# Gate and up projections of three FFNs as seven block products instead of eight

## The chip, the cores and the metric

The kernel runs on one core of one Trainium2 chip. The metric is the time on the device, in microseconds, from the start to the end of one execution. The core has a matrix engine (TensorE; PE in the views, with its weight loads as PEld) and three engines for everything else: VectorE (DVE), ScalarE (ACT) and GpSimd (POOL). SyncE (SP) issues most DMAs, GpSimd issues the rest. The engines run side by side, each one its own queue of instructions in order, and wait for one another by semaphores.

## The reference

Two layers of a transformer block over 512 image tokens (A) and 256 context tokens (C), width 1024, all in float32. Each layer has two FFNs of inner width 2816 around a stage of four mixers:

```python
def swiglu(h, wg, wu, wd):
    return (jax.nn.silu(h @ wg) * (h @ wu)) @ wd
...
    for i in range(DEPTH):
        need_ctx = i < DEPTH - 1
        mx = modulation(c, ada_w[i], ada_b[i])
        mc = modulation(c_ctx[None, :], ada_w[i], ada_b[i])
        x = x + 0.5 * mx[2] * swiglu(pre_norm(x, norm1_g[i], mx[0], mx[1]), ffn1_wg[i], ffn1_wu[i], ffn1_wd[i])
        xc = xc + 0.5 * mc[2] * swiglu(pre_norm(xc, norm1_g[i], mc[0], mc[1]), ffn1_wg[i], ffn1_wu[i], ffn1_wd[i])
        ...
        x = x + mx[5] * (jnp.concatenate([ya, yd, ym, yn], axis=-1) @ w_out[i])
        x = x + 0.5 * mx[8] * swiglu(pre_norm(x, norm3_g[i], mx[6], mx[7]), ffn2_wg[i], ffn2_wu[i], ffn2_wd[i])
        if need_ctx:
            ...
```

So four FFNs run one behind the other. Three of them are on image and context together: both of layer 0 and the first of layer 1. The last one is on the image alone. `modulation` is a product of a vector with a 1024 x 9216 matrix; its nine slices (j = 0 to 8) scale, shift and gate the norms and FFNs.

## The kernel before

Activations lie transposed, with the 1024 features as KD = 8 chunks of 128 partitions and the tokens along the free dimension. Every large product is done as three float32r matmuls (`mm3`, lines 290 to 292): each operand is split into a rounded high part and the rest (hi by ScalarE at L269, lo = src - hi by VectorE at L274), and high x high, high x low and low x high are added in PSUM.

`ffn` loops over 22 blocks f of 128 hidden features. For a block it loads the gate and the up weights (two tiles `wr` of 128 x 1024, by SyncE), splits them, and runs 8 chunks x 3 matmuls x 2 (gate and up) on the context (256 columns, bank `guC`) and on the image (512 columns, banks `gA`, `uA`). ScalarE makes silu of the gate (L326), VectorE multiplies (L327) and both split the result into `hh` and `hl`. After every group of 5 or 6 blocks (`GROUPS`) the down projection runs: for each of 8 chunks m of output features a weight tile is loaded and split, the matmuls of the group go to `dacc`, and VectorE adds the result, scaled by the gate column, into the residual X (L348). In the last group this is done token part by token part (`PASSES`), so that the norm of a part (`norm`, L260, L263, L264: `nt`, then `xnh` and `xnl`) can run while the next part is multiplied.

The modulation runs beside the FFNs as a generator (`ada`) of which `fill` takes a few steps per block: GpSimd's queue loads weight tiles `adaw` (L133), and VectorE multiplies each by two columns and accumulates into four tiles `adaacc` (L159, L161). `adasum` adds them over the partitions on TensorE.

The program is written in this order, and a scheduler of the framework places the instructions of each engine by a timeline of its own; the order on the chip is fixed when the program is built.

## Time and profile before

| what | value |
|---|---|
| time, median of 3 runs | 3256.35 us (3253.59 to 3258.81) |
| the profiled execution: its time | 3254.35 us |
| its span, first to last instruction | 3252.6 us |
| mean granted TensorE clock | 0.977 of full speed |
| PE, DVE, ACT, POOL busy | 96%, 53%, 33%, 14% of the span |

Times of a timeline are counted from the start of the span. A matmul's duration runs into that of the next (they are pipelined), so the price of a matmul in a stream is the distance between two starts. In the same way two VectorE instructions overlap by some hundredths of a microsecond where neither waits.

### The profile page before, as it was taken

How to read it: one execution, taken by the hardware profiler on the slowest of the kernel's cores; microseconds unless marked ns; L12 is line 12 of the kernel's file. 1: busy time of each engine (PE TensorE's matmuls, PEld its weight loads, DVE VectorE, ACT ScalarE, POOL GpSimd, SP SyncE). 2: the span in 40 equal slices, each digit the busy share in tenths (PEclk: the TensorE clock that was granted, in tenths of full speed). 3: DMA queues.
4: the chain of work that ended last, by engine and by line, in shares of the span. 5: the costliest groups of instructions: out<-in, count | busy, mean ns of one | idle time of the engine just before them, and what ended most of it. 6: DMA issues, size and time to landing. Idle time of an engine off the chain costs nothing.

```text
span 3252.6 us, 48912 instructions
## 1 busy us (share of the span) xinstructions
PE 3129.6 (96%) x19586; PEld 2713.3 (83%) x19586; DVE 1715.9 (53%) x3044; ACT 1069.6 (33%) x1927; POOL 463.6 (14%) x772
## 2 busy tenths in 40 slices
PE   7999999998999999999999999999997899999998
PEld 4888888886788889888889988888886688788887
DVE  5746354836855477675736332322746744353334
ACT  3212112555444433121224212122455353342223
POOL 2201010411232021121102000000311322000001
PEclk9999999999999999999999999999998999899999
DMA  6534242514533354454424221212523623323333
GB/s 244 153 104 138 87 117 81 168 62 124 159 91 87 89 191 131 142 153 126 128 77 123 63 64 59 72 53 67 148 78 114 162 57 81 121 86 96 97 97 104
DMA packets 135396, 357.45 MB, mean 110 GB/s; under 512 B 20000, under 2 KB 33824, under 8 KB 134912
## 3 DMA queue, kind: packets, MB, share of 16 engines
q1 hardware_dynamic: 101056, 255.47, 25.9%
q0 software_dynamic: 34112, 98.85, 11.0%
q8 instruction: 154, 2.52, 0.3%
q14 instruction: 74, 0.61, 0.1%
HBM read 316.89 MB, written 39.65 MB: 110 GB/s over the span
## 4 chain that ended last, share of the span: by engine, by line
PE 57%; DVE 4%; issue 3%; DMA 2%; ACT 1%; POOL 0%; POOLq 0%; DVEq 0%; SPq 0%; ACTq 0%
PE dacc L290 4%; PE dacc L292 4%; PE dacc L291 4%; PE gA L290 4%; PE gA L291 4%; PE uA L290 4%; PE uA L292 4%; PE uA L291 4%; PE gA L292 4%; PE guC L292 3%; PE guC L290 3%; PE guC L291 3%; PE o L740 2%; PE pj L290 1%; PE pj L292 1%
## 5 line engine op out<-in xcount | busy, mean ns | idle before, releaser
L269 ACT CAST wh<-wr 128x1024 fp32r<-128x1024 f32 (+5 forms) x443 | 394.7, 893 | 1239.4 <-PE dacc L291 453.3
L274 DVE TENSOR_TENSOR wl<-wr,wh 128x1024 fp32r<-128x1024 f32 (+5 forms) x443 | 461.2, 1043 | 422.6 <-ACT wh L269 391.6
L290 PE MATMUL dacc<-hh,wh 128*128 128x256 f32 (+1 forms) x1392 | 452.5, 326 | 2.2 <-ACT wh L269 1.9
L292 PE MATMUL dacc<-hh,wl 128*128 128x256 f32 (+1 forms) x1392 | 450.4, 326 | 3.6 <-DVE wl L274 3.5
L291 PE MATMUL dacc<-hl,wh 128*128 128x256 f32 (+1 forms) x1392 | 452.2, 326 | 0.0
L161 DVE SCALAR_TENSOR_TENSOR adaacc<-adaw,silc,adaacc 128x512 f32<-128x512 f32 x448 | 315.4, 748 | 12.2 <-DMA adaw<-ada_w 11.8
L290 PE MATMUL guC<-xnhC,wh 128*128 128x256 f32 x1056 | 300.2, 285 | 1.6 <-ACT xnhC L263 1.5
L291 PE MATMUL guC<-xnlC,wh 128*128 128x256 f32 x1056 | 299.5, 284 | 1.5 <-DVE xnlC L264 1.5
L292 PE MATMUL guC<-xnhC,wl 128*128 128x256 f32 x1056 | 299.0, 283 | 0.5 <-DVE wl L274 0.5
L290 PEld LDWEIGHTS dacc<-hh,wh 128*128 128x128 f32 x1392 | 261.4, 188 | 32.0 <-ACT wh L269 6.1
L290 PE MATMUL gA<-xnhA,wh 128*128 128x512 f32 (+1 forms) x752 | 284.8, 379 | 1.7 <-ACT xnhA L263 1.7
L292 PEld LDWEIGHTS dacc<-hh,wl 128*128 128x128 f32 x1392 | 261.0, 188 | 29.6 <-DVE wl L274 5.0
L290 PE MATMUL uA<-xnhA,wh 128*128 128x512 f32 (+1 forms) x752 | 283.0, 376 | 0.6 <-ACT wh L269 0.6
L292 PE MATMUL uA<-xnhA,wl 128*128 128x512 f32 (+1 forms) x752 | 282.8, 376 | 0.7 <-DVE wl L274 0.7
L291 PE MATMUL uA<-xnlA,wh 128*128 128x512 f32 (+1 forms) x752 | 282.9, 376 | 0.0
L292 PE MATMUL gA<-xnhA,wl 128*128 128x512 f32 (+1 forms) x752 | 282.8, 376 | 0.0
L291 PE MATMUL gA<-xnlA,wh 128*128 128x512 f32 (+1 forms) x752 | 282.2, 377 | 0.0
L291 PEld LDWEIGHTS dacc<-hl,wh 128*128 128x128 f32 x1392 | 261.4, 188 | 24.6
L133 POOL DMA_DIRECT2D adaw<-ada_w x256 | 140.6, 550 | 799.2 <-DVE adaacc L159 483.3
L348 DVE SCALAR_TENSOR_TENSOR xA<-dacc,modG,xA 128x512 f32<-128x512 f32 (+1 forms) x160 | 101.9, 640 | 239.3 <-PE dacc L292 239.2
L290 PEld LDWEIGHTS guC<-xnhC,wh 128*128 128x128 f32 x1056 | 202.7, 192 | 9.5 <-ACT wh L269 5.2
L291 PEld LDWEIGHTS guC<-xnlC,wh 128*128 128x128 f32 x1056 | 202.6, 192 | 4.4 <-DVE xnlC L264 2.0
(354 smaller groups left out, 5944.9 us busy)
## 6 DMA issues: line engine op xcount, KB each, us to landing
wr<-wgu SPq DMA_DIRECT2D x176, 512.0 KB, 3.6
adaw<-ada_w POOLq DMA_DIRECT2D x256, 256.0 KB, 3.3
wr<-wd SPq DMA_DIRECT2D x120, 320.0 KB, 3.0
wr<-wd SPq DMA_DIRECT2D x64, 384.0 KB, 3.2
wr<-win SPq DMA_DIRECT2D x44, 512.0 KB, 3.9
...
```

The costliest lines, as they stand in the source:

```text
L133: load = lambda q, t, k, c: q.dma_start(out=t, in_=self.I["ada_w"][l, k * 128:(k + 1) * 128, c:c + 512])
L161: nc.vector.scalar_tensor_tensor(out=t, in0=w, scalar=c, in1=t, op0=ALU.mult, op1=ALU.add)
L269: nc.scalar.copy(hi, src)
L274: (nc.vector if leng == "V" else nc.gpsimd).tensor_tensor(lo, src, hi.bitcast(F32), op=ALU.subtract)
L290: nc.tensor.matmul(out, lhsT=wh, rhs=xh, start=start, stop=False)
L291: nc.tensor.matmul(out, lhsT=wh, rhs=xl, start=False, stop=False)
L292: nc.tensor.matmul(out, lhsT=wl, rhs=xh, start=False, stop=stop)
L348: nc.vector.scalar_tensor_tensor(out=x, in0=acc, scalar=gate[:, i, m, r:r + 1], in1=x, op0=ALU.mult, op1=ALU.add)
L740: nc.tensor.matmul(o[:, q0 + q], lhsT=p[:, q * 128:q * 128 + 128], rhs=v(kb), start=False, stop=kb == 3 and q == n // 128 - 1)
```

## The change

In the three FFNs on image and context, the two projections of a block f are taken as one product of 2 x 2 blocks: the rows are gate and up, the inner dimension is the two halves of the 1024 features (4 chunks each), and the columns are two halves of the tokens (256 image tokens and 128 context tokens each, 384 columns). Strassen's scheme in Winograd's form makes it from seven products instead of eight: `chunk7` yields after each product; a product is 4 chunks x 3 matmuls x 384 columns. Three banks a, b, c of PSUM hold the sums. Of the weights four sums (`ws`, 128 x 512) are made for each block, on GpSimd; seven blocks of 128 x 512 are split instead of two of 128 x 1024. The results take nine VectorE instructions of 384 columns for a block. The sums of the activations (`T7`, and one that overwrites a quarter of `XN`) are made once for each FFN, in `sums7`; while they are made the first block, f = 0, is multiplied in the old way with 256 columns at a time.

`ffn2` runs the steps of neighbouring blocks interleaved (`order`), and the down projection in groups of 3 blocks (the last of 4). Of the modulation one of the two multiplications goes to ScalarE (product) and GpSimd (sum, L201 of the changed kernel); it has 3 buffers for its weights instead of 6, runs over two more stages (the last six slices of layer 1 now beside the first FFN of layer 1), and takes other steps per block (`FILL`). The last FFN keeps the old way. The projections into the mixers read the image in two halves.

The diff, cut to its core:

```diff
-NS, LAG = [0, 2, 2, 2], 2
+LAG = 2
+RB, BB, WAIT = 4, 5, 3
+GROUPS2 = [(f, f + 3) for f in range(0, 18, 3)] + [(18, 22)]
+SLOTS = 7
...
-        self.XNh, self.XNl = {}, {}
-        for q, t in self.T.items():
-            self.XNh[q] = p.tile([128, KD, t], F32R, name="xnh" + q)
-            self.XNl[q] = p.tile([128, KD, t], F32R, name="xnl" + q)
+        self.XN = {w: [p.tile([128, 4, 2, 384], F32R, name="xn%s%d" % (w, i)) for i in range(2)] for w in "hl"}
+    def xn(self, w, u, k):
+        return self.tok(self.XN[w][k // 4][:, k % 4], u)
+    def tok(self, t, u):
+        return {"A": t[:, :, 0:256], "C": t[:, :, 256:384], "A0": t[:, 0, 0:256], "A1": t[:, 1, 0:256]}[u]
...
-                    for v in range(2):
-                        t, c = acc[2 * g + v], self.silc[:, k, v:v + 1]
-                        if k == 0:
-                            nc.vector.tensor_scalar(out=t, in0=w, scalar1=c, scalar2=None, op0=ALU.mult)
-                        else:
-                            nc.vector.scalar_tensor_tensor(out=t, in0=w, scalar=c, in1=t, op0=ALU.mult, op1=ALU.add)
+                    t, c = acc[2 * g:2 * g + 2], [self.silc[:, k, v:v + 1] for v in range(2)]
+                    if k == 0:
+                        nc.vector.tensor_scalar(out=t[0], in0=w, scalar1=c[0], scalar2=None, op0=ALU.mult)
+                        nc.scalar.activation(t[1], w, ACTF.Copy, scale=c[1])
+                    else:
+                        nc.vector.scalar_tensor_tensor(out=t[0], in0=w, scalar=c[0], in1=t[0], op0=ALU.mult, op1=ALU.add)
+                        nc.scalar.activation(w, w, ACTF.Copy, scale=c[1])
+                        nc.gpsimd.tensor_tensor(t[1], t[1], w, op=ALU.add)
                 yield
...
+    def block(self, src):
+        w = src.shape[-1]
+        hi = self.wp.tile([128, 512], F32R, tag="bh", name="wh", bufs=BB)
+        lo = self.wp.tile([128, 512], F32R, tag="bl", name="wl", bufs=BB)
+        self.split(src, hi[:, :w], lo[:, :w])
+        return hi, lo
...
+    def ffn2(self, l, i, fill, save, then):
+        nc = self.nc
+        fi = 0 if i == 0 else 1
+        up, dn, gate = self.I["wgu"], self.I["wd"], self.modG
+        H = {}
+        def hid(f):
+            H[f] = [self.hp.tile([128, 768], F32R, tag=t, name=t).rearrange("p (h t) -> p h t", h=2) for t in ("hh", "hl")]
+            return H[f]
+        W = [self.weight(up[l, fi, 0, :, j], 1024) for j in range(2)]
+        temps = {kk: [self.hp.tile([128, 768], F32, tag=t, name="x" + t).rearrange("p (k c) -> p k c", k=2)
+                      for t in ("hh", "hh", "hl", "hl")] for kk in (0, 2)}
+        hh, hl = hid(0)
+        for u in self.units(["A", "C"]):
+            gu = self.psum((128, 2, TC), name="gu", ring="p")
+            for j in range(2):
+                wh, wl = W[j]
+                for k in range(KD):
+                    self.mm3(self.two(gu[:, j], u), wh[:, k * 128:(k + 1) * 128], wl[:, k * 128:(k + 1) * 128],
+                             self.xn("h", u, k), self.xn("l", u, k), k == 0, k == KD - 1)
+            sg = self.fs.tile([128, 384], F32, tag="sg", name="sg")[:, :TC]
+            h = self.fs.tile([128, 384], F32, tag="s1", name="h")[:, :TC]
+            nc.scalar.activation(sg, gu[:, 0], ACTF.Silu)
+            nc.vector.tensor_tensor(h, sg, gu[:, 1], op=ALU.mult)
+            self.split(self.two(h, u), self.tok(hh, u), self.tok(hl, u))
+        self.sums7(temps)
+        def down(f0, f1, m, us, last):
+            while (l, 3 * i + 2) not in self.adone:
+                self.fill(1)
...
+        order = sorted((SLOTS * (f - 1) + 2 * n, f, n) for f in range(1, NF) for n in range(SLOTS))
+        chunks, tasks, gi = {}, [], 0
+        for t, f, n in order:
+            if n == 0:
+                chunks[f] = self.chunk7(up[l, fi, f], hid, f)
+            next(chunks[f], None)
+            if n == SLOTS - 1 and f == GROUPS2[gi][1] - 1 and f < NF - 1:
+                tasks += [(t + WAIT, *GROUPS2[gi], m) for m in range(KD)]
+                gi += 1
+            if tasks and tasks[0][0] <= t:
+                down(*tasks.pop(0)[1:], ("C", "A"), False)
+            if n in fill:
+                self.fill(1)
+        for k in tasks:
+            down(*k[1:], ("C", "A"), False)
+        due = []
+        for us in PASSES[2]:
+            for m in range(KD):
+                if due and m >= LAG:
+                    then(due.pop(0))
+                down(*GROUPS2[-1], m, us, True)
+            due += us
+        for u in due:
+            then(u)
+    def sums7(self, temps):
+        nc = self.nc
+        self.T7 = {w: [self.tp7.tile([128, 4, 384], F32R, name="t%s%d" % (w, n)) for n in range(3)] for w in "hl"}
+        for c in (slice(256, 384), slice(0, 256)):
+            for kk in (0, 2):
+                ks = slice(kk, kk + 2)
+                x12, x22, x11, x21 = [t[:, :, c] for t in temps[kk]]
+                for x, i, j, e in ((x12, 0, 1, nc.vector), (x22, 1, 1, nc.vector), (x11, 0, 0, nc.gpsimd), (x21, 1, 0, nc.gpsimd)):
+                    e.tensor_tensor(x, *[self.XN[w][i][:, ks, j, c].bitcast(F32) for w in "hl"], op=ALU.add)
+                nc.vector.tensor_tensor(x11, x12, x11, op=ALU.subtract)
+                nc.vector.tensor_tensor(x12, x22, x12, op=ALU.subtract)
+                nc.vector.tensor_tensor(x22, x22, x11, op=ALU.subtract)
+                nc.gpsimd.tensor_tensor(x21, x21, x22, op=ALU.subtract)
+                for x, n in ((x22, 1), (x11, 0), (x12, 2)):
+                    self.split(x, *[self.T7[w][n][:, ks, c] for w in "hl"])
+                self.split(x21, *[self.XN[w][0][:, ks, 1, c] for w in "hl"])
+    def chunk7(self, ap, hid, f):
+        nc = self.nc
+        raw = []
+        for j in range(2):
+            t = self.wp.tile([128, 1024], F32, tag="wr", name="wr", bufs=RB)
+            nc.sync.dma_start(out=t, in_=ap[:, j])
+            raw += [t[:, 0:512], t[:, 512:1024]]
+        A11, A12, A21, A22 = raw
+        T = lambda n: [self.T7[w][n] for w in "hl"]
+        B = lambda i, j: [self.XN[w][i][:, :, j] for w in "hl"]
+        s = lambda: self.wp.tile([128, 512], F32, tag="ws", name="ws", bufs=4)
+        small = lambda tag: self.fs.tile([128, 384], F32, tag=tag, name=tag)
+        def product(bank, src, x, first):
+            wh, wl = self.block(src)
+            for k in range(4):
+                c = slice(k * 128, k * 128 + 128)
+                self.mm3(bank, wh[:, c], wl[:, c], x[0][:, k], x[1][:, k], first and k == 0, k == 3, True)
+        add = lambda e, o, a, b, op=ALU.add: e.tensor_tensor(o, a, b, op=op)
+        a = self.psum((128, 384), name="pa", ring="p")
+        product(a, A11, B(0, 0), True)
+        s1 = small("s1")
+        nc.scalar.copy(s1, a)
+        yield
+        b = self.psum((128, 384), name="pb", ring="p")
+        S1, S2 = s(), s()
+        add(nc.gpsimd, S1, A21, A22)
+        add(nc.gpsimd, S2, S1, A11, ALU.subtract)
+        product(b, S2, T(1), True)
+        u2 = small("u2")
+        add(nc.vector, u2, b, s1)
+        yield
+        c = self.psum((128, 384), name="pc", ring="p")
+        product(c, S1, T(0), True)
+        add(nc.gpsimd, S2, A12, S2, ALU.subtract)
+        yield
+        S3 = s()
+        add(nc.gpsimd, S3, A11, A21, ALU.subtract)
+        product(b, S3, T(2), False)
+        u3 = small("u3")
+        add(nc.vector, u3, b, s1)
+        add(nc.vector, u3, c, u3)
+        yield
+        product(a, A12, B(1, 0), False)
+        sg = small("sg")
+        nc.scalar.activation(sg, a, ACTF.Silu)
+        yield
+        product(c, S2, B(1, 1), False)
+        add(nc.vector, u2, c, u2)
+        nc.scalar.activation(u2, u2, ACTF.Silu)
+        hh, hl = hid(f)
+        add(nc.vector, u3, u2, u3, ALU.mult)
+        self.split(u3, hh[:, 1], hl[:, 1])
+        yield
+        product(b, A22, B(0, 1), False)
+        add(nc.vector, s1, b, s1)
+        add(nc.vector, s1, sg, s1, ALU.mult)
+        self.split(s1, hh[:, 0], hl[:, 0])
...
-                    self.side = self.ada(1)
+                    self.side = chain(self.ada(0, 8, 9), self.ada(1, 0, 3))
...
-                self.ffn(l, 0, both, FILL[0] if l == 0 else 0, parts, then, NS[2 * l])
+                if l == 1:
+                    self.side = self.ada(1, 3, 9)
+                self.ffn2(l, 0, FILL[l], parts, then)
...
-        self.ffn(l, 2, parts, FILL[1] if l == 0 else 0, (), then, NS[2 * l + 1])
+        if l == 0:
+            self.ffn2(l, 2, FILL[1], (), then)
+        else:
+            self.ffn(l, 2, then, 2)
...
-FILL = (2, 3)
+FILL = ((0, 2, 4, 6), (0, 2, 4))
```

What the scheduler made of it is shown on three engines.

TensorE, in the middle of the first FFN, before: the context's last matmuls of a block and the image's first (L290 to L292 are the three of `mm3`).

```order
L290 MATMUL guC<-xnhC,wh 128x256
L291 MATMUL guC<-xnlC,wh 128x256
L292 MATMUL guC<-xnhC,wl 128x256
L290 MATMUL guC<-xnhC,wh 128x256
L291 MATMUL guC<-xnlC,wh 128x256
L292 MATMUL guC<-xnhC,wl 128x256
L290 MATMUL gA<-xnhA,wh 128x512
L291 MATMUL gA<-xnlA,wh 128x512
L292 MATMUL gA<-xnhA,wl 128x512
L290 MATMUL gA<-xnhA,wh 128x512
```

The same engine and stage in the changed kernel: the end of one product (first product of a block, into its bank a, on a half of `XN`) and the start of another (the fifth of the block ahead of it). Products of neighbouring blocks alternate.

```order
L351 MATMUL pa<-xnh_128,wh 128x384
L352 MATMUL pa<-xnl_130,wh 128x384
L353 MATMUL pa<-xnh_128,wl 128x384
L351 MATMUL pa<-xnh_129,wh 128x384
L352 MATMUL pa<-xnl_131,wh 128x384
L353 MATMUL pa<-xnh_129,wl 128x384
L351 MATMUL pa<-xnh_129,wh 128x384
L352 MATMUL pa<-xnl_131,wh 128x384
L353 MATMUL pa<-xnh_129,wl 128x384
```

Each matmul now has 384 columns, and a product of 12 stands whole where no down projection runs.

VectorE, at the start of the first FFN, before: the end of the norm (`nt`, `xnl`), then the modulation and the first results.

```order
L260 SCALAR_TENSOR_TENSOR nt<-xC,modA_74,rb 128x256 x2
L264 SCALAR_TENSOR_TENSOR xnlA<-nt,mod_72,xnhA 128x512 x2
L264 SCALAR_TENSOR_TENSOR xnlC<-nt,mod_72,xnhC 128x256
L260 SCALAR_TENSOR_TENSOR nt<-xA,modA_74,rb 128x512
L264 SCALAR_TENSOR_TENSOR xnlC<-nt,mod_72,xnhC 128x256
L260 SCALAR_TENSOR_TENSOR nt<-xA,modA_74,rb 128x512
L264 SCALAR_TENSOR_TENSOR xnlA<-nt,mod_72,xnhA 128x512 x2
L159 TENSOR_SCALAR adaacc<-adaw,silc 128x512 x4
L327 TENSOR_TENSOR h_410<-sg,guC 128x256
L161 SCALAR_TENSOR_TENSOR adaacc<-adaw,silc,adaacc 128x512 x2
L274 TENSOR_TENSOR wl<-wr,wh 128x1024
```

VectorE at the same start in the changed kernel, behind the norms: the sums of the activations (L494 to L497, tiles `xhh`, `xhl`) and the low parts of their splits (`tl` for th + tl = T7). The row `tl_658` of 128x2x256 here is the last part of the sum that the second product of every block reads.

```order
L497 TENSOR_TENSOR xhh<-xhh,xhl 128x2x128
L199 SCALAR_TENSOR_TENSOR adaacc<-adaw,silc,adaacc 128x512
L319 TENSOR_TENSOR tl_659<-xhh,th_656 128x2x128
L497 TENSOR_TENSOR xhh<-xhh,xhl 128x2x256
L319 TENSOR_TENSOR xnl_130<-xhl,xnh_128 128x2x256
L319 TENSOR_TENSOR tl_659<-xhh,th_656 128x2x256
L319 TENSOR_TENSOR wl<-wr,wh 128x512
L434 TENSOR_TENSOR h<-sg,gu 128x256
L319 TENSOR_TENSOR tl_658<-xhh,th_655 128x2x128
L319 TENSOR_TENSOR tl_658<-xhh,th_655 128x2x256
L319 TENSOR_TENSOR xnl_130<-xhl,xnh_128 128x2x128
```

Between the norm and the first results there are now the sums, and weight splits (`wl`) among them.

VectorE in the middle of the first FFN in the changed kernel, where the down projection (`wd`) begins; `u_`, `s_` are the results of products (L525), `pb` and `pc` their banks.

```order
L525 TENSOR_TENSOR u_3202<-pc,u_3202 128x384
L319 TENSOR_TENSOR wl<-wr,wh 128x512
L525 TENSOR_TENSOR u_3303<-u_3202,u_3303 128x384
L525 TENSOR_TENSOR s_3085<-pb,s_3085 128x384
L319 TENSOR_TENSOR wl<-wr,wh 128x512
L525 TENSOR_TENSOR s_3085<-sg,s_3085 128x384
L319 TENSOR_TENSOR hl<-u_3303,hh 128x384
L196 TENSOR_SCALAR adaacc<-adaw,silc 128x512
L525 TENSOR_TENSOR u_3378<-pb,s_3327 128x384
L196 TENSOR_SCALAR adaacc<-adaw,silc 128x512
L319 TENSOR_TENSOR hl<-s_3085,hh 128x384
L319 TENSOR_TENSOR wl<-wd,wh 128x384
```

Splits of weights for later products stand between the results of earlier ones. GpSimd in the same stage, where before only the loads `adaw<-ada_w` stood: `ws` are the sums of weights.

```order
L201 TENSOR_TENSOR adaacc<-adaacc,adaw 128x512
L168 DMA adaw<-ada_w 128x512
L525 TENSOR_TENSOR ws<-wr 128x512
L201 TENSOR_TENSOR adaacc<-adaacc,adaw 128x512 x2
L525 TENSOR_TENSOR ws<-ws,wr 128x512
L525 TENSOR_TENSOR ws<-wr 128x512
L168 DMA adaw<-ada_w 128x512
L201 TENSOR_TENSOR adaacc<-adaacc,adaw 128x512
L168 DMA adaw<-ada_w 128x512 x2
L201 TENSOR_TENSOR adaacc<-adaacc,adaw 128x512
```

The sums of weights and the sums of the modulation now stand in one queue with its loads.

## Rows read from the trace of the kernel before

**Rows 1.** The page: busy time of each engine; PE in 40 slices.
```profile
PE 3129.6 (96%) x19586; PEld 2713.3 (83%) x19586; DVE 1715.9 (53%) x3044; ACT 1069.6 (33%) x1927; POOL 463.6 (14%) x772
...
PE   7999999998999999999999999999997899999998
```

**Rows 2.** Busy time of each engine in four windows (us).
```profile
40.00:60.00 20.00, 17.02 (x94) 13.77 (x93) 17.32 (x34) 10.06 (x17) 0.00 (x0) 1.00 0.12 50
320.00:400.00 80.00, 80.00 (x465) 70.46 (x464) 33.96 (x49) 14.33 (x20) 3.81 (x7) 1.00 0.32 99
1220.00:1240.00 20.00, 20.00 (x168) 19.26 (x167) 12.20 (x27) 10.27 (x18) 0.70 (x1) 1.00 0.04 5
1820.00:1840.00 20.00, 20.00 (x126) 18.11 (x125) 7.11 (x9) 5.51 (x8) 0.00 (x0) 1.00 0.17 54
```

**Rows 3.** Groups by shape, whole run: TensorE matmuls of the FFNs; busy us, mean ns.
```profile
L290 PE MATMUL guC<-xnhC,wh 128*128 128x256 f32 x1056 | 300.2, 285 | 1.6 <-ACT xnhC L263 1.5
...
L290 PE MATMUL gA<-xnhA,wh 128*128 128x512 f32 x656 | 256.9, 392 | 0.8 <-ACT xnhA L263 0.8
...
L290 PE MATMUL dacc<-hh,wh 128*128 128x256 f32 x848 | 238.8, 282 | 2.2 <-ACT wh L269 1.9
...
L290 PE MATMUL dacc<-hh,wh 128*128 128x512 f32 x544 | 214.9, 396 | 0.0
```

**Rows 4.** Timeline of PE, first FFN, 271 to 305 us: start, duration.
```profile
271.79 0.28 PE L290 MATMUL guC<-xnhC,wh 128*128 128x256 f32 x1
...
276.35 0.28 PE L292 MATMUL guC<-xnhC,wl 128*128 128x256 f32 x1
...
299.73 0.39 PE L292 MATMUL uA<-xnhA,wl 128*128 128x512 f32 x1
...
303.81 0.39 PE L292 MATMUL uA<-xnhA,wl 128*128 128x512 f32 x1
```

**Rows 5.** Timeline of VectorE in the first FFN: start, duration.
```profile
42.91 0.87 DVE L260 SCALAR_TENSOR_TENSOR nt<-xC,modA,rb 128x256 f32<-128x256 f32 x2
43.70 1.40 DVE L260 SCALAR_TENSOR_TENSOR nt<-xA,modA,rb 128x512 f32<-128x512 f32 x2
...
82.64 0.68 DVE L327 TENSOR_TENSOR h<-sg,uA 128x512 f32<-128x512 f32 x1
83.24 0.42 DVE L274 TENSOR_TENSOR hl<-h,hh 128x256 fp32r<-128x256 f32 x1
83.58 1.41 DVE L161 SCALAR_TENSOR_TENSOR adaacc<-adaw,silc,adaacc 128x512 f32<-128x512 f32 x2
...
86.04 1.40 DVE L161 SCALAR_TENSOR_TENSOR adaacc<-adaw,silc,adaacc 128x512 f32<-128x512 f32 x2
87.37 0.68 DVE L274 TENSOR_TENSOR hl<-h,hh 128x512 fp32r<-128x512 f32 x1
```

**Rows 6.** Timeline of VectorE, 590 to 600 us.
```profile
594.33 1.77 DVE L274 TENSOR_TENSOR wl<-wr,wh 128x640 fp32r<-128x640 f32 x1
...
596.42 0.81 DVE L274 TENSOR_TENSOR wl<-wr,wh 128x640 fp32r<-128x640 f32 x1
```

**Rows 7.** Timeline of GpSimd, 590 to 600 us.
```profile
594.67 0.74 POOL L226 TENSOR_TENSOR ssA<-ssA,sq 128x256 f32<-128x256 f32 x1
```

**Rows 8.** Groups by shape of GpSimd, whole run.
```profile
L133 POOL DMA_DIRECT2D adaw<-ada_w x256 | 140.6, 550 | 799.2 <-DVE adaacc L159 483.3 <-DVE adaacc L161 237.5 <-PE ytr L763 53.2
...
L1223 POOL TENSOR_TENSOR MT<-dni,egn 128x128 f32<-128x128 f32 x48 | 18.1, 401 | 34.5 <-PE sp L1266 19.4 <-issue 15.1
...
L1242 POOL TENSOR_TENSOR P<-Qt,eg 128x256 f32<-128x256 f32 x20 | 12.1, 613 | 4.0 <-PE pt L1246 1.9 <-DVE m L666 1.1 <-DVE ov L1303 0.6
L581 POOL TENSOR_TENSOR mqu<-rt,rt 32x512 f32<-32x512 f32 x8 | 11.1, 1386 | 87.6 <-DVE rt L580 72.4 <-issue 15.2
```

**Rows 9.** Groups by shape, whole run: one of ScalarE, one of VectorE.
```profile
L161 DVE SCALAR_TENSOR_TENSOR adaacc<-adaw,silc,adaacc 128x512 f32<-128x512 f32 x448 | 315.4, 748 | 12.2 <-DMA adaw<-ada_w 11.8
...
L269 ACT CAST hh<-h 128x512 fp32r<-128x512 f32 x88 | 54.7, 622 | 26.2 <-DVE h L327 24.2
```

191 lines of the change are left out of this document (116 added, 75 removed).

## The prediction

> **What bounds the kernel now.** First the shares of busy time on the page, then the slices of TensorE: TensorE is busy 96% of the span, VectorE 53%, ScalarE 33%, GpSimd 14%, and nearly every slice of PE reads 9 [rows 1]. Then four windows. In the middle of the first FFN TensorE is busy 80.00 of 80 us while VectorE has 33.96 and GpSimd 3.81 [rows 2]. Where the three FFNs begin it has 17.02, 20.00 and 20.00 of 20; only at the very start is there idle time, beside a VectorE that is busy 17.32 of 20. So in these FFNs a matmul less is time less, as long as the other engines keep up. The granted clock is 1.00 in all four windows, so no clock loss is priced.
>
> The sum is made against the profiled execution: 3254.35 us, 2 us under the median of 3256.35. About 0.2% (6.5 us) is what a measurement can tell from no change.
>
> **Removed: an eighth of the gate and up work.** The durations of matmuls in the groups, 285 ns with 256 columns and 392 with 512 [rows 3], contain the overlap with the next; the price of one in a stream is the distance of two starts. 256 columns: (276.35 - 271.79)/38 = 0.120 us; 512 columns: (303.81 - 299.73)/18 = 0.2267 us [rows 4]. No row has 384 columns; the line through both gives 0.1733. Bounds: three quarters of 512 (0.170) and one and a half of 256 (0.180). A block took 48 x 0.2267 + 48 x 0.120 = 16.64 us and takes 84 x 0.1733 = 14.56: 2.08 less. With 21 blocks in three FFNs that is 131. Block 0 now takes 144 x 0.120 = 17.28: 0.64 more in the first FFN; the other two had blocks 0 and 1 in this form already and save 0.64 each at block 1. Net **-132** (bounds -149 and -97). The down projection has the same matmuls; its smaller groups only add results.
>
> **Added at the start of three FFNs.** From the second product on every block reads T7, which VectorE makes behind the norms. Before T7 is whole, TensorE has, by the order, the 144 matmuls of block 0 and 55 others: 17.3 + 55 x 0.1733 = 26.8 us. VectorE's pitches [rows 5]: a norm step of 256 columns 0.395 (two in 0.79), an operation on two tensors of 512 columns 0.60, of 256 0.34, an accumulation of 512 0.665 (1.33 for two; 0.748 as the mean duration of a single one over the run [rows 9]). In the first FFN, from 42.9 us on: 48 norm steps x 0.395 = 19.0; 17 pieces of 512 and 17 of 256 for the sums and their splits 10.2 + 5.8 = 16.0; five weight splits of 512 3.0; results of block 0 1.7; modulation 1.5 and small ones 0.9. That is 42; with 5 for half of 14 additions on GpSimd (their hold is told below) and 3 for ScalarE's turns in the splits, T7 is whole some 50 us after 42.9, at about 93. TensorE has 27 of these 50 covered and, as before, waited some 3 anyway: about 20 more. In the second FFN there are 57 us on VectorE against 34 on TensorE (26.8 and 7 of the stage ahead), 23; in the third, where the residual adds and the modulation stand between, 70 against 43, 27. Before, these two starts had no idle time [rows 2]. Sum **+70**. Bounds: 40 (no holds, splits fully side by side) and 100.
>
> **Added in the steady state.** A period is three blocks with their down projection: TensorE 3 x 14.56 + 72 x (0.120 + 0.2267) + 1 = 69.6 us. VectorE in it, 384 columns taken halfway between 256 and 512 (0.47): 21 weight splits 12.6, eight splits of `wd` 3.8, 27 results 12.7, 16 residual adds 8.5 and, with a slice of the modulation, 14 x 0.665 + 0.8 = 10.1; in all 47.7. This alone fits. GpSimd had next to no additions; now 12 sums of weights and 14 of the modulation, 128x512 each. No row has this form: the line through 128x128 (401 ns) and 128x256 (613 ns) gives 1.04 us, 32x512 took 1.386 [rows 8]; I take 1.15, nearer the line, since it has the same partitions. With 16 loads at 0.55 [rows 8] GpSimd has 39 of 69.6 us. ScalarE has some 60 operations at most 0.62 each [rows 9]: 37.
>
> The two engines are not independent. A split of 128x640 on VectorE took 1.77 us [rows 6] while a GpSimd addition of 0.74 ran [rows 7], and the next one without company 0.81: the addition held VectorE for about its own length. The Trainium skill ("SBUF — State Buffer", Who interferes with whom) states the same: a VectorE instruction with two SBUF inputs and a GpSimd instruction exclude one another for whole instructions. The trace agrees in this one case.
>
> The eight working steps of a slice fall into two blocks in the first FFN (four steps a block; three steps behind them do nothing) and into 2.67 in the others. In the two dense blocks VectorE has (47.7 - 10.1) x 2/3 + 10.1 = 35.2 us of its own, GpSimd 22 additions, TensorE 46.3. If no addition holds VectorE nothing is lost; if all 22 do, at 1.15, VectorE needs 60.5 and a slice loses 14.2. In the others: 43.5 of VectorE, 24.7 additions, 61.8 of TensorE, and 10.1 lost at worst. Six slices and 9.25: between 0 and 85 + 93 = 178. VectorE spends 24 of 46 us in operations on two SBUF tensors, so about half of the additions meet one, and some more hold the one that comes next: I take 0.6. Then 35.2 + 15.2 = 50.4 against 46.3, 4.1 x 6 = 24; in the others 60.5 against 61.8, nothing. With 6 for slots with a down projection **+30**. Against moving sums to GpSimd speaks the Trainium skill ("GPSIMD Engine Reference", 4.1 Engine selection): elementwise work belongs to VectorE, GpSimd being about half as fast; its 2.6 cycles for an element (3.1) would make an addition 1.1 us, an estimate that changes no term.
>
> **Small ones.** Mixer projections read the image in halves: 12 x (48 x 0.120 - 24 x 0.2267) = **+4**. The additions into the sums of squares keep their places: 0.
>
> **Sum.** 3254.4 - 132 + 70 + 30 + 4 = 3226, 0.8% under the run's own time.
>
> **Rivals.**
> - Slower: GpSimd's additions hold VectorE in the slices. With a share of 0.8: 35.2 + 20.2 = 55.4, 9.1 x 6 = 55, and 43.5 + 22.7 = 66.2, 4.4 x 9.25 = 41: 96 in place of 30, 3292; at worst 3374. It decides from 132 - 70 - 4 = 58 us on, a share of about 0.7 (40 + 15). For it speaks the 1.77, which is more than 0.81 and 0.74 together; against it that results that read PSUM, and the residual adds, have only one SBUF input.
> - Faster: the holds are hidden and T7 comes at its lower bound: 3254.4 - 132 + 40 + 4 = 3166. For it speaks that VectorE alone has 48 of 70 us and that five split blocks are buffered, about 7 us of products (three and a half of 2.08).
> - No gain in the matmul: 384 columns cost one and a half of 256, 0.180. Then 3254.4 - 97 + 104 = 3261, just beyond what can be told. Against it: a line through two points of the same stream is a plain model.
>
> **Chances.** Forecast 0.48 (its own range 3190 to 3246), faster rival 0.21, slower rival 0.22, matmul price 0.09. Some of the forecast's upper end and half of the last lie within 0.2%. So faster 0.68, same 0.10, slower 0.22. For 8 in 10 the range takes the faster rival's middle and most of the slower one: 3155 to 3292.
>
> **What would show it.** Right: a pitch of 0.173 us between matmuls of 384 columns; idle TensorE of about 20 us before the first matmul on T7 in each of three FFNs, ended by the split that makes `tl`; TensorE busy over 95% in blocks without modulation and some 4 us lost in a slice; additions on GpSimd near 1.15 us, and VectorE operations beside them longer by that. Wrong: TensorE waiting for `wl` in every block, a pitch of 0.18, or VectorE waiting for `adaw`. There are three buffers now and a tile passes VectorE, ScalarE and GpSimd before it is free; if that takes over three times the 2.9 us between tiles (46.3/16), VectorE waits for the load with the splits queued behind it, which no term holds.

## The result and the profile after

The changed kernel takes 3415.26 us (median of 4 runs, 3409.57 to 3424.16) against 3257.54 for the kernel before: a ratio of 1.0489, 95% interval 1.0463 to 1.0515. It is slower by nearly 5%, where 0.8% faster was forecast, and lies beyond the whole range. The profiled execution, the longest of the four, has a span of 3422.4 us, 169.8 more than that of before.

The page of the changed kernel: busy time of the engines, then TensorE and its granted clock in 40 slices.

```profile
PE 3127.6 (91%) x19000; PEld 2779.1 (81%) x19000; DVE 2306.8 (67%) x3777; ACT 1420.3 (41%) x2718; POOL 1208.6 (35%) x1296
...
PE   5899999889899996999999799999989799999998
...
PEclk8899999989999997999999899999999899899999
```

Against [rows 1], VectorE goes from 1715.9 to 2306.8 us and GpSimd from 463.6 to 1208.6. TensorE is busy for 3127.6 us, where it was 3129.6: the matmuls saved are gone and its busy time has fallen by 2 us. The slices of the clock show 8 and 7 where the three FFNs begin (1 and 2, 16, 23) and 8 in the mixers (9, 32, 35).

The kernel before by stages, in windows: first FFN, mixers of layer 0, second and third FFN. Columns: window, its length, busy time of PE, PEld, DVE, ACT, POOL (with instructions), mean granted clock, share and GB/s of the DMA.

```profile
40.00:617.00 577.00, 571.84 (x3392) 497.31 (x3390) 342.39 (x541) 146.53 (x234) 91.62 (x162) 1.00 0.41 123
617.00:1207.00 590.00, 554.57 (x4083) 484.36 (x4082) 345.40 (x743) 269.98 (x566) 133.35 (x221) 0.96 0.41 116
1207.00:2344.00 1137.00, 1132.28 (x6916) 1006.28 (x6914) 568.76 (x901) 292.93 (x472) 111.94 (x179) 1.00 0.34 100
```

The same stages of the changed kernel.

```profile
40.00:682.00 642.00, 576.42 (x3162) 520.18 (x3161) 517.77 (x748) 267.53 (x499) 338.79 (x322) 0.95 0.34 103
682.00:1303.00 621.00, 574.15 (x4230) 508.50 (x4230) 347.39 (x745) 285.36 (x600) 157.20 (x239) 0.93 0.38 109
1303.00:2512.00 1209.00, 1109.53 (x6284) 1019.37 (x6282) 993.00 (x1441) 509.34 (x957) 578.72 (x517) 0.97 0.32 95
```

Idle time of TensorE is the length less its busy time. In the three FFNs it was 5.2 + 4.7 = 9.9 us and is 65.6 + 99.5 = 165; VectorE is busy 81% and 82% of these stages, where it was 59% and 50%. The FFNs are 65 + 72 = 137 us longer, the mixers of layer 0 31.

The pitch, from a timeline of TensorE where nothing waits (34 matmuls of 384 columns, the first and the last).

```profile
1641.16 0.34 PE L353 MATMUL pa<-xnh,wl 128*128 128x384 f32 x1
...
1646.95 0.33 PE L353 MATMUL pa<-xnh,wl 128*128 128x384 f32 x1
```

(1646.95 - 1641.16)/33 = 0.1755 us: the line gave 0.1733. Over 63 x 84 matmuls the difference is 12 us, so the work saved is 120 to 132 us, as forecast.

The three starts, 83 us each, in the changed kernel.

```profile
49.00:132.00 83.00, 64.79 (x326) 59.29 (x326) 77.08 (x129) 37.25 (x77) 48.46 (x48) 0.77 0.16 50
1301.00:1384.00 83.00, 57.34 (x312) 51.49 (x311) 81.67 (x133) 40.77 (x80) 47.24 (x44) 0.81 0.24 73
1901.00:1984.00 83.00, 59.01 (x327) 53.13 (x326) 81.42 (x120) 39.05 (x78) 50.74 (x46) 0.81 0.28 84
```

TensorE idles 18.2 + 25.7 + 24.0 = 67.9 us in them. The same windows of the kernel before (from 41, 1204 and 1823 us) have 5.0, so 63 came in; 7 more of a wait of 8.00, shown below, lie just ahead of the first window. That makes the 70 that was forecast. Yet it is not T7 that TensorE waits for. Its waits in the first start (us in total, times, longest):

```profile
PE rb L281 <- DVE dg L277: 8.0, 1, 8.0
PE gu L352 <- DVE xnl L309: 6.3, 5, 2.2
PE pa L353 <- DVE wl L319: 2.6, 1, 2.6
PE gu L351 <- ACT xnh L308: 2.4, 4, 1.0
PE pb L352 <- DVE tl L319: 2.3, 1, 2.3
```

Only the last of these is on `tl`; in the second start there is no such wait, in the third one of 0.4. The sums stand on VectorE between the norm steps and the weight splits, and so it is `xnl` and `wl` that come late, inside block 0 already. The longest wait has another cause, seen in a timeline of all engines (in brackets: idle time ahead of the instruction, and what ended it).

```profile
46.22 1.26 POOL L525 TENSOR_TENSOR ws<-wr 128x512 f32<-128x512 f32 x1 [9.60 <-DMA wr<-wgu]
47.44 0.72 POOL L290 TENSOR_TENSOR rsr<-rsv,mhalf 128x2 f32<-128x2 f32 x1
...
48.19 1.48 DVE L277 TENSOR_TENSOR dg<-ident,rsr 128x256 f32<-128x256 f32 x1 [4.54 <-POOL rsr L290]
...
49.82 0.77 PE L281 MATMUL rb<-dg,ones 128*128 128x256 f32 x1 [8.00 <-DVE dg L277]
```

GpSimd's first sum of weights waits 9.60 us for the weights to land; the small power `rsr`, which the norm needs, stands behind it in GpSimd's queue, then `dg` on VectorE, then `rb` on TensorE: 8.00 us lost before the first FFN begins, where the longest such wait was 1.2 before. Before, that queue held no sum of weights [rows 8].

The first FFN behind its start, in three stretches: with modulation slices at work, without them, and behind its last product (the rest of the down projection).

```profile
135.00:524.00 389.00, 357.90 (x1915) 318.83 (x1915) 332.43 (x433) 166.18 (x299) 238.53 (x219) 0.97 0.38 116
524.00:634.00 110.00, 110.00 (x634) 103.78 (x633) 71.18 (x116) 38.38 (x71) 23.76 (x16) 1.00 0.19 57
634.00:682.00 48.00, 40.47 (x272) 35.20 (x272) 31.02 (x60) 21.70 (x47) 24.55 (x37) 0.96 0.57 176
```

With slices at work VectorE is busy 85% and TensorE loses 31 us. Without them, at 65%, it loses nothing. Behind the last product it loses 7.5. Cut in the same way, the three FFNs lose 66 us in 936 with slices at work (VectorE 87%), 1 in 515 without (68%), and 21 behind the last products, where the kernel before lost 4. No share of VectorE's time is a limit by itself. The kernel before, in the densest 100 us of its second FFN, had VectorE at 84% and lost nothing:

```profile
1400.00:1500.00 100.00, 100.00 (x581) 85.17 (x580) 84.44 (x136) 21.26 (x33) 25.52 (x47) 1.00 0.60 176
```

Groups of GpSimd and VectorE, whole run: busy us, mean ns, idle time before.

```profile
L201 POOL TENSOR_TENSOR adaacc<-adaacc,adaw 128x512 f32<-128x512 f32 x224 | 329.3, 1478 | 184.5 <-ACT adaw L200 184.0
L525 POOL TENSOR_TENSOR ws<-wr 128x512 f32<-128x512 f32 x126 | 184.3, 1463 | 383.8 <-DMA wr<-wgu 356.0 <-DVE u L525 12.0 <-DVE wl L319 9.0
```

```profile
L319 DVE TENSOR_TENSOR wl<-ws,wh 128x512 fp32r<-128x512 f32 x252 | 235.7, 942 | 21.5 <-ACT wh L314 21.2
L199 DVE SCALAR_TENSOR_TENSOR adaacc<-adaw,silc,adaacc 128x512 f32<-128x512 f32 x224 | 232.5, 1045 | 44.4 <-DMA adaw<-ada_w 43.9
...
L319 DVE TENSOR_TENSOR hl<-u,hh 128x384 fp32r<-128x384 f32 x63 | 65.8, 1044 | 4.4 <-ACT hh L314 4.2
```

An addition takes 1.46 to 1.51 us on the mean (1.25 the shortest), where 1.15 was taken. A split of 512 columns takes 0.94 us, where a single one takes 0.68, and `hl` of one half of the tokens 1.04, where 0.55 is the shortest kind: VectorE is held. How far that goes is shown by timelines of VectorE and of GpSimd at the first start.

```profile
90.13 4.95 DVE L494 TENSOR_TENSOR xhh<-xnh,xnl 128x512 f32<-128x512 f32 x1
...
89.96 0.83 POOL L494 TENSOR_TENSOR xhl<-xnh,xnl 128x256 f32<-128x256 f32 x1
90.76 1.28 POOL L498 TENSOR_TENSOR xhl<-xhl,xhh 128x512 f32<-128x512 f32 x1
92.01 1.29 POOL L494 TENSOR_TENSOR xhl<-xnh,xnl 128x512 f32<-128x512 f32 x1
93.27 1.25 POOL L525 TENSOR_TENSOR ws<-wr 128x512 f32<-128x512 f32 x1
```

An addition of VectorE of 512 columns, 0.68 us long in [rows 5], takes 4.95 us while four additions of GpSimd run one behind the other from 89.96 to 94.52. It ends 0.56 us behind the last of them: VectorE gets no turn between them. The Trainium skill ("SBUF — State Buffer", Who interferes with whom) says that a VectorE instruction with two SBUF inputs and a GpSimd instruction that reads SBUF exclude one another for whole instructions. This agrees, and the rows show that it can go on over several in a row.

### The profile page after: what moved, and what is told of

Its sections match the earlier page's. It is cut to its first block, busy times and chain, and to the rows that moved or that the text cites. A ratio compares the mean times of both kernels' runs of the same rounds, so it can differ in the third digit from the quotient of the medians.

```text
span 3422.4 us, 50556 instructions
## 1 busy us (share of the span) xinstructions
PE 3127.6 (91%) x19000; PEld 2779.1 (81%) x19000; DVE 2306.8 (67%) x3777; ACT 1420.3 (41%) x2718; POOL 1208.6 (35%) x1296
## 5 line engine op out<-in xcount | busy, mean ns | idle before, releaser
L319 DVE TENSOR_TENSOR wl<-wr,wh 128x512 fp32r<-128x512 f32 (+4 forms) x365 | 363.1, 1000 | 197.3 <-ACT wh L314 184.6
L314 ACT CAST wh<-wr 128x512 fp32r<-128x512 f32 (+4 forms) x365 | 265.6, 734 | 506.1 <-PE dacc L352 151.1
L201 POOL TENSOR_TENSOR adaacc<-adaacc,adaw 128x512 f32<-128x512 f32 x224 | 329.3, 1478 | 184.5 <-ACT adaw L200 184.0
L525 POOL TENSOR_TENSOR ws<-wr 128x512 f32<-128x512 f32 x126 | 184.3, 1463 | 383.8 <-DMA wr<-wgu 356.0
L200 ACT ACTIVATE adaw<-adaw,silc 128x512 f32<-128x512 f32 x224 | 161.2, 723 | 300.9 <-DVE adaacc L199 269.9
L351 PE MATMUL pj<-xnh,wh 128*128 128x256 f32 (+2 forms) x768 | 254.9, 333 | 14.6 <-ACT wh L314 12.0
L199 DVE SCALAR_TENSOR_TENSOR adaacc<-adaw,silc,adaacc 128x512 f32<-128x512 f32 x224 | 232.5, 1045 | 44.4 <-DMA adaw<-ada_w 43.9
L353 PE MATMUL pj<-xnh,wl 128*128 128x256 f32 (+2 forms) x768 | 249.2, 327 | 10.7 <-DVE wl L319 10.6
L319 DVE TENSOR_TENSOR wl<-ws,wh 128x512 fp32r<-128x512 f32 x252 | 235.7, 942 | 21.5 <-ACT wh L314 21.2
L352 PE MATMUL pj<-xnl,wh 128*128 128x256 f32 (+2 forms) x768 | 250.0, 326 | 0.0
L319 DVE TENSOR_TENSOR wl<-wd,wh 128x384 fp32r<-128x384 f32 (+1 forms) x224 | 169.5, 757 | 52.8 <-ACT wh L314 50.9
L353 PE MATMUL pa<-xnh,wl 128*128 128x384 f32 x504 | 173.6, 349 | 21.1 <-DVE wl L319 21.1
```

What stands on the lines that cost most here:

```text
L199: nc.vector.scalar_tensor_tensor(out=t[0], in0=w, scalar=c[0], in1=t[0], op0=ALU.mult, op1=ALU.add)
L200: nc.scalar.activation(w, w, ACTF.Copy, scale=c[1])
L201: nc.gpsimd.tensor_tensor(t[1], t[1], w, op=ALU.add)
L314: nc.scalar.copy(hi, src)
L319: (nc.vector if leng == "V" else nc.gpsimd).tensor_tensor(lo, src, hi.bitcast(F32), op=ALU.subtract)
L351: nc.tensor.matmul(out, lhsT=wh, rhs=xh, start=start, stop=False, skip_group_check=more)
```

## The experiments

All are edits of the changed kernel, but for e12. Four runs of each except e13 (five), on a chip beside the kernel before. VectorE's busy time and TensorE's idle time are those of the three FFNs, from the windows by stage of each profile; a profiled execution can lie some way from the median (e13's lies 17 us above it, e2's 12 below).

| kernel | median us | ratio to before (95%) | VectorE busy | TensorE idle |
|---|---|---|---|---|
| before | 3257 | 1 | 911 | 10 |
| the changed kernel | 3415.3 | 1.0489 (1.0463 to 1.0515) | 1511 | 165 |
| e1 modulation on VectorE | 3397.7 | 1.0423 (1.0393 to 1.0452) | 1503 | 160 |
| e2 no additions on GpSimd | 3385.9 | 1.0381 (1.0354 to 1.0408) | 1483 | 143 |
| e3 without one column of modulation | 3330.7 | 1.0218 (1.0194 to 1.0242) | 1351 | 117 |
| e4 without sums of activations | 3352.9 | 1.0279 (1.0240 to 1.0319) | 1427 | 127 |
| e5 two old blocks | 3422.7 | 1.0510 (1.0491 to 1.0528) | 1510 | 173 |
| e6 e2 with two old blocks | 3383.8 | 1.0383 (1.0361 to 1.0405) | 1469 | 162 |
| e7 e6, modulation in finer steps | 3383.0 | 1.0395 (1.0369 to 1.0422) | 1470 | 162 |
| e8 e7, weight sums on GpSimd | 3409.3 | 1.0467 (1.0449 to 1.0485) | 1499 | 173 |
| e9 e2, modulation held back at the starts | 3367.5 | 1.0339 (1.0322 to 1.0357) | 1499 | 135 |
| e10 e9 with two old blocks | 3360.9 | 1.0323 (1.0306 to 1.0340) | 1479 | 122 |
| e11 without sums and modulation | 3224.8 | 0.9907 (0.9883 to 0.9932) | 999 | 59 |
| e13 without modulation | 3270.7 | 1.0048 (1.0031 to 1.0064) | 1223 | 84 |
| e14 without weight sums | 3344.3 | 1.0273 (1.0258 to 1.0288) | 1357 | 123 |

**Holds or own work: e1, e2, e3, e13, e14.** Theory A said that GpSimd's additions cost through the holds; theory B that VectorE is late by its own work. e1:

```diff
-                        nc.scalar.activation(w, w, ACTF.Copy, scale=c[1])
-                        nc.gpsimd.tensor_tensor(t[1], t[1], w, op=ALU.add)
+                        nc.vector.scalar_tensor_tensor(out=t[1], in0=w, scalar=c[1], in1=t[1], op0=ALU.mult, op1=ALU.add)
```

> Changed kernel with both columns of the modulation on VectorE, as in the kernel before; GpSimd keeps only the loads and the 12 sums of weights for three blocks. Theory A (an addition on GpSimd holds VectorE: VectorE's instructions ran 372 us longer than their shortest forms over the three FFNs, 0.78 us for each of 476 additions): 224 additions less free about 175 us of VectorE, 224 accumulations more cost 149 at 0.665, so VectorE gains little and the time falls by 10 to 50 us, to 3365 to 3405. Theory B (VectorE is late through its own work and order, the holds cost nothing): VectorE has 149 us more, the time rises by 30 to 100, to 3445 to 3515.

3397.7, inside A's range; B falls. e2 moves the weight sums too:

```diff
-        add(nc.gpsimd, S1, A21, A22)
+        add(nc.vector, S1, A21, A22)
...
-        add(nc.gpsimd, S3, A11, A21, ALU.subtract)
+        add(nc.vector, S3, A11, A21, ALU.subtract)
```

> As the one before, and the four sums of weights of a block on VectorE too, so that GpSimd has no additions in the blocks. Theory A: 476 holds of 0.78 (372 us) go and 224 x 0.665 + 252 x 0.60 = 300 come; in two dense blocks VectorE has 49 us against 52 before and nothing stretches, so idle time of TensorE and the low clock behind it fall: 3300 to 3380. Theory B: VectorE has 300 us more, the time rises by 80 or more, above 3495.

3385.9: no rise, so B is out, but 6 us outside A's range too. Its windows by stage:

```profile
40.00:659.00 619.00, 567.10 (x3164) 512.28 (x3165) 513.19 (x927) 210.29 (x403) 96.59 (x154) 0.97 0.36 108
...
1261.00:2469.00 1208.00, 1116.68 (x6278) 1019.22 (x6277) 969.42 (x1750) 423.26 (x812) 152.35 (x227) 0.96 0.33 96
```

GpSimd is down to 97 and 152 us, and a split of 512 columns takes 0.70 us on the mean instead of 0.94: VectorE is no longer held. Yet VectorE is as busy as before (1483 against 1511), and TensorE idles 143 us instead of 165. What the holds took, VectorE now spends on the additions. A share over a whole stage hides where VectorE is short; here is the first FFN of e2 with slices at work and without.

```profile
150.00:390.00 240.00, 222.74 (x1197) 192.30 (x1197) 227.59 (x402) 69.53 (x131) 39.74 (x74) 0.99 0.47 138
400.00:600.00 200.00, 200.00 (x1150) 190.21 (x1149) 136.14 (x244) 69.34 (x128) 0.00 (x0) 1.00 0.21 63
```

With slices at work VectorE is busy 95% and TensorE loses 17 us in 240; without them, at 68%, it loses nothing. VectorE's own waits for TensorE's results and for ScalarE's high parts (`dacc` 33.6, `wh` 23.0, `pb` 15.8 us from 130 to 640 us) lie nearly all behind 400 us, where they cost nothing. e3 and e13 leave out parts of the modulation:

```diff
-                        nc.scalar.activation(w, w, ACTF.Copy, scale=c[1])
-                        nc.gpsimd.tensor_tensor(t[1], t[1], w, op=ALU.add)
```

> Leaves out the second column of the modulation but for its first step (ScalarE's product and GpSimd's sum for k over 0), so gates and shifts of the context are not the reference's; VectorE's own work is unchanged. Theory A: in two dense blocks VectorE needs 35.2 + 8 x 0.78 = 41 us, under TensorE's 46.3; of the some 80 us idle in steady state about 60 go, and most of the 75 us that the lower clock costs there: 3260 to 3320. Theory B: the holds cost nothing, so 3395 to 3420.

3330.7, 11 us above A's range, and far from B's. e13 leaves out the accumulation of the other column as well:

```diff
-                        nc.vector.scalar_tensor_tensor(out=t[0], in0=w, scalar=c[0], in1=t[0], op0=ALU.mult, op1=ALU.add)
```

> Leaves out all steps of the modulation but the first in the blocks (e3 left out one column's), sums of weights and of activations stay; the output is not the reference's. Against e3 VectorE is relieved of 224 accumulations more (149 us) and of no more holds. If VectorE's whole occupancy, own work and holds alike, is what TensorE waits for: 30 to 60 us less than e3, 3270 to 3300. If the holds are the cause and own work is covered: within 15 us of e3, 3315 to 3345.

3270.7: 60 us less than e3, so VectorE's own work counts as its holds do. e14:

```diff
-        add(nc.gpsimd, S1, A21, A22)
-        add(nc.gpsimd, S2, S1, A11, ALU.subtract)
+        S1, S2, S3 = A21, A11, A22
...
-        product(c, S2, B(1, 1), False)
+        product(c, A12, B(1, 1), False)
```

> Leaves out the sums of the weights alone (products take quarters of the weights as they are, so the output is not the reference's); modulation and sums of activations stay. Occupancy: VectorE is relieved of some 0.78 x 252 = 197 us of holds, close to the 175 of e3: 60 to 90 us less than the changed kernel, 3325 to 3355. If what costs in the modulation is its chain of three engines and its loads with three buffers, and not the holds: less than 40 us, 3375 or more.

3344.3, 71 us less than the changed kernel, as occupancy said: the weight sums cost about what one column of the modulation does (85). Whichever of these is taken off, TensorE's idle time falls with VectorE's busy time, from 165 at 1511 through 117 to 127 at 1351 to 1427 and 84 at 1223 to 59 at 999. Holds and own work count about alike: 85 us of time for 160 less of VectorE in e3, 71 for 154 in e14, 60 for 128 in e13 against e3. Only the last takes work from VectorE alone; e3 and e14 relieve ScalarE and GpSimd too. The order counts as well, since e6, e9 and e10 scatter (162, 135 and 122 at 1469 to 1499). So theory A was right that the holds cost, and too narrow: it is VectorE's occupancy, held or own, where slices are at work and at the starts.

That is not the whole condition, as the kernel before lost nothing at 84%. One thing that it had more of is work split ahead: three buffers of 1024 columns for the high and for the low parts of its weights, some 25 us of its products by their pitch, against five of 512, some 10 us. Whether more buffers would let the changed kernel bear it was not tried; e12 shows what one buffer less did to the kernel before.

**The starts: e4, e5, e6, e9, e10.** e4:

```diff
-        self.sums7(temps)
...
-        T = lambda n: [self.T7[w][n] for w in "hl"]
+        T = lambda n: [self.XN[w][1][:, :, n % 2] for w in "hl"]
```

> Leaves out the sums of the activations at the start of the three FFNs (the products read quarters of the normed activations in their place), so the output is not the reference's. If the starts are late through these sums: TensorE's idle time there (77 us more than before in the three starts) falls to about 25 and the time at the lower clock (46 us more) to about 15, so the time falls by 70 to 95, to 3320 to 3345. Rival: the starts are late through the queue of GpSimd (the first wait of 8 us there) and the norms themselves, which stay: the time falls by less than 30, to 3385 or more.

3352.9, 62 less; 8 us short of the first case and far from the rival. In the three starts 37.6 us of idle time stay of 67.9, and ahead of them the wait behind GpSimd's queue stays too (`rb` still waits 6.2 us). e5 gives TensorE a second old block to work on:

```diff
+        for f in range(OLD):
+            if f:
+                W = [self.weight(up[l, fi, f, :, j], 1024) for j in range(2)]
...
-        order = sorted((SLOTS * (f - 1) + 2 * n, f, n) for f in range(1, NF) for n in range(SLOTS))
+        order = sorted((SLOTS * (f - OLD) + 2 * n, f, n) for f in range(OLD, NF) for n in range(SLOTS))
```

> Changed kernel with blocks 0 and 1 of the three FFNs in the old way, so that TensorE has 17.3 us more of work that needs no sums of activations; it gives up 2.7 us x 3 of the saving. If the starts are late because VectorE has norms and sums to make at once: idle time there falls from 74 us to 20 to 40, and the low clock behind it with it: 3340 to 3380. Rival: the idle time sits in the norms themselves, which the second old block needs too, and in splits that wait: 3400 to 3425.

3422.7, the rival's range. The same on e2:

> e2 (no additions on GpSimd in the blocks) with two old blocks. Same two theories, on a kernel whose VectorE is not stretched: 3310 to 3345 if the starts are the demand on VectorE, 3370 to 3395 if not. If the holds of GpSimd at the start matter, this one gains more than e5 over its base.

3383.8: no gain here either. A timeline of VectorE in e6 at the first start says why (start, duration, xcount):

```profile
89.13 3.77 DVE L200 SCALAR_TENSOR_TENSOR adaacc<-adaw,silc,adaacc 128x512 f32<-128x512 f32 x3
92.83 3.05 DVE L496 TENSOR_TENSOR xhh<-xnh,xnl 128x256 f32<-128x256 f32 x4
...
109.74 3.21 DVE L200 SCALAR_TENSOR_TENSOR adaacc<-adaw,silc,adaacc 128x512 f32<-128x512 f32 x4
...
126.53 2.89 DVE L200 SCALAR_TENSOR_TENSOR adaacc<-adaw,silc,adaacc 128x512 f32<-128x512 f32 x2
...
137.86 0.68 DVE L318 TENSOR_TENSOR tl<-xhh,th 128x512 fp32r<-128x512 f32 x1
```

Accumulations of the modulation (L200) now stand between and before the sums (L496), and the last low part `tl` comes at 137.86, where in the changed kernel it came at about 105. The scheduler filled the cover with other work. e9 and e10 hold this back:

```diff
-                    if l == 0 and j == 2 and k < WB // 2:
+                    if (l, j) in ((0, 2), (0, 8), (1, 3)) and k < WB // 2:
...
-                        nc.gpsimd.tensor_copy(w[:, 0:1], self.xn("l", "A1", KD - 1)[:, 0:1].bitcast(F32))
+                        nc.gpsimd.tensor_copy(w[:, 0:1], self.T7["l"][1][:, 3, 255:256].bitcast(F32))
```

> e2 with the first loads of the modulation in each of the three FFNs held back until the last sum of the activations is split (the small copy on GpSimd that holds them waits for it), so that no accumulation stands between the norms and the sums on VectorE. If the starts are VectorE's demand there (norms, sums and some 20 accumulations): the three starts lose 20 to 40 us of idle time and as much low clock: 3320 to 3365. If modulation there costs nothing: 3380 to 3395.

3367.5: 18 us less than e2, between the two cases.

> e9 with two old blocks. In e6 the second old block brought nothing, and its trace shows accumulations of the modulation on VectorE in place of the sums while TensorE worked on it; with these held back it covers the sums: 20 to 50 us less than e9, 3280 to 3340. If it is the old block itself that delays the sums (its splits and results): within 10 us of e9.

3360.9: within 10 us of e9. TensorE idles 13 us less, but the second old block gives up some 8 us of the saving. At the first start the last `tl` comes at 119.0, where it comes at 100.1 in e9, so the old block delays the sums by about as much as it covers. It is the fastest kernel here that computes the reference, and still 3% slower than before.

**Even filling: e7, e8.**

```diff
                     for v in range(2):
...
-                yield
+                    yield
...
-FILL = ((0, 2, 4, 6), (0, 2, 4))
+FILL = ((0, 1, 2, 3, 4, 5, 6), (0, 1, 2, 3, 4, 5), (0, 2, 4, 6))
```

> e6 with the modulation in single weight tiles, one in a step, and steps in nearly every product, so that the same work lies evenly over the stage in place of two dense blocks out of three. If TensorE is late in the blocks through the density of VectorE's work in some of them: idle time there falls from some 60 us to 20, the low clock with it, 60 to 80 us less than e6. If it is late through the order inside a block (results that wait for a bank, splits queued behind them): within 15 us of e6.

3383.0, but this tells nothing of density: on VectorE the order came out row for row as in e6. The scheduler places the steps by its own timeline, whatever the generator yields. e7 is a second measurement of e6, 0.8 us from it.

> e7 with the sums of weights back on GpSimd. If GpSimd's additions, once the modulation is off it, hold VectorE for longer (0.78 us each) than they save it (0.60): up to 40 us slower than e7. If they are hidden in an evenly filled stage: 10 to 40 us faster than e7.

3409.3, 26 us more than e7: here a weight sum costs more on GpSimd than on VectorE.

**The bare products: e11** has the edits of e4 and e14, and of the modulation the first step alone, on VectorE.

> Leaves out the sums of the activations, the sums of the weights (products take quarters of the weights as they are) and all steps of the modulation but the first, so the output is not the reference's; TensorE's matmuls, the splits and the nine results of a block are those of the changed kernel. If what VectorE, ScalarE and GpSimd have to do beside is the whole loss: TensorE idles as little as in the kernel before, 3254 - 132 + 10: 3125 to 3160. If the chain inside a block (bank, result, split, each on another engine in order) loses time of its own: some 40 us idle in the blocks and as much at the low clock remain, 3180 to 3230.

```profile
40.00:613.00 573.00, 547.24 (x3171) 506.81 (x3168) 335.90 (x642) 201.84 (x388) 82.69 (x143) 0.98 0.38 116
...
1216.00:2321.00 1105.00, 1071.47 (x6280) 1002.73 (x6278) 663.45 (x1260) 405.15 (x781) 121.33 (x202) 0.99 0.35 104
```

3224.8, in the second range. Of the 132 us that TensorE saves, 31 are left, although the modulation, which the kernel before has, is gone and nothing is added to VectorE but the nine results and the seven smaller splits of a block. Its 59 us of idle time are in part still at the starts (12.5), 22 lie behind the last products, and the rest at single places, such as residual adds that wait at the first down projections (a bank of `dacc`, 3.9 us at most). The chain inside a block, as that case put it, loses nothing that the waits show: from 250 to 570 us the profile lists no wait of TensorE.

**What a wait costs: e12** is the kernel before with a small shortage.

```diff
-        self.weights(e("wp", 3, self.side_x), 1024)
+        self.weights(e("wp", 2, self.side_x), 1024)
```

> The kernel before with two buffers of each kind for FFN weights in place of three, so that TensorE waits at times in an FFN, with nothing else changed. If idle time takes the granted clock down with it: the time lost beyond the idle time itself, by the count of matmuls at their prices, is 0.5 to 1 of the idle time, and the granted clock of those stretches falls under 1.00. If the low clock of the changed kernel came from its matmul shapes or its order: idle time here costs itself alone and the clock stays at 1.00 in the FFNs. If two buffers do not make TensorE wait, it tells nothing.

It takes 3338.4 us, a ratio of 1.0253 (1.0237 to 1.0270). VectorE's busy time in the three FFNs is 921 us, where it was 911, so the 82 us are the price of one buffer less and not of VectorE's work. The second and third FFN in a window:

```profile
1234.00:2414.00 1180.00, 1156.11 (x6913) 1009.87 (x6913) 572.57 (x909) 294.08 (x476) 114.59 (x179) 1.00 0.32 96
```

Idle time went from 4.7 to 23.9 us, and busy time, for the same matmuls, from 1132.3 to 1156.1. The mean clock reads 1.00 in both. So neither case came as put: time beyond the idle time is lost, about as much again, but not through the clock. A timeline of TensorE in this window shows where it is.

```profile
1799.34 0.28 PE L291 MATMUL dacc<-hl,wh 128*128 128x256 f32 x1
1799.97 0.39 PE L292 MATMUL dacc<-hh,wl 128*128 128x256 f32 x1 [0.36 <-DVE wl L274]
1800.20 0.28 PE L290 MATMUL dacc<-hh,wh 128*128 128x256 f32 x1
1800.32 0.28 PE L291 MATMUL dacc<-hl,wh 128*128 128x256 f32 x1
1800.43 0.28 PE L292 MATMUL dacc<-hh,wl 128*128 128x256 f32 x1
```

In the stream a matmul of 256 columns starts every 0.12 us. Here the next start is 1799.97 - 1799.34 = 0.63 us later, 0.51 lost, of which the profile shows 0.36 as a wait: the last matmul ahead of it counts as busy to its end, 0.28. Behind the wait the pitch is 0.23 once, 0.11 more. A wait that reads 0.36 costs 0.62, and a delay of under 0.16 us (0.28 less 0.12) shows as no idle time at all.

## Why the prediction was wrong

| term | forecast us | the runs |
|---|---|---|
| matmuls saved | -132 | -120 to -132, by the pitch |
| idle time at three starts | +70 | +70 |
| idle time in the blocks | +30 (0 to 178) | +66 with slices at work, about 2 elsewhere |
| idle time behind the last products | 0 | +17 |
| busy time of the FFNs beyond the matmuls | 0 | +114 (-18 instead of -132) |
| mixers | +4 | +34 |

These make +171 with -132 in the first line; the span grew by 169.8. Three terms failed by size, the busy time (+114 against 0), the blocks (+66 against +30) and the mixers (+34 against +4), and one was left out, the idle time behind the last products.

- **The matmuls** were right.
- **The starts** were right in size and wrong in place. The waits are for norms and splits delayed by the sums, and 8 us of them are GpSimd's queue, which the prediction looked at for holds alone and not for what stands behind a waiting sum.
- **The blocks: sums set against sums.** The prediction took a loss to be VectorE's sum less TensorE's (50.4 against 46.3, and 60.5 against 61.8: nothing). The holds in it were right, by luck. Compared with e2 group by group, VectorE's instructions took 331 us longer over 476 additions, 0.69 us each, and 0.6 x 1.15 is 0.69; but an addition took 1.47 us and held VectorE for about half of that. (The 0.78 of e1's expectation was counted against the shortest forms.) What failed is the subtraction. With slices at work TensorE lost 66 us beside a VectorE that was busy only 87%: it was late while it had time left, since it waits too, from 150 to 550 us for `adaw` (19.6 us) and for high parts (12.8). In e2, where it is busy 95%, the subtraction is nearly right: 49 us against 46.3 is 5.5 lost in 100, and the rows show 7. The slower rival (96 in place of 30) had the mechanism, the holds; e2 shows that taking them away by putting the work on VectorE gives back only 29 us, as VectorE then spends the time itself.
- **Behind the last products: a term put at nothing.** "The down projection has the same matmuls; its smaller groups only add results." TensorE idles 21 us there, where it idled 4, and waits for splits of `wd`; e2 and e11 show the same. Why these come later than before was not taken apart.
- **The busy time: no price for the clock and for what surrounds a wait.** "The granted clock is 1.00 in all four windows, so no clock loss is priced" held for the kernel before only. With a mean clock of 0.95 and 0.97, up to 0.05 x 576 + 0.03 x 1110 = 62 of the 114 us are the clock, more than half of it in the starts, where it reads 0.77 to 0.81 (0.23 x 65 + 0.19 x 116 = 37). Counted over the distances between starts of all matmuls of these stages, those that begin at the lower of the clock's two levels take some 50 us more than at the upper. At the upper level the distances hold some 50 us more beyond the idle time shown than before: 36 around waits, and 13 in delays too short to show as idle, the two kinds that e12 has. Up to 12 is the pitch. Several expectations call all of it "low clock"; e12 shows that this was too simple.
- **The mixers** were 31 us longer in the first stage, with the clock at 0.93 instead of 0.96. In other runs with the same projections that stage took 601 to 623. What moves it was not tried and stays open.
- The wait of VectorE for `adaw`, named as a risk, is there: 43.9 us against 11.8 in [rows 9].

The question of the change was where its gain of 132 us went: it was made in full on TensorE, and given back twice over in the same FFNs, somewhat more than half as idle time that the profile shows (155), the rest as lower clock and delays that it counts as busy (114).
